# Layer 0 experts: three nested levels of token rounds per expert in place of eight, with the tokens beyond the 192nd in a block behind the last expert

## The chip, the cores and the metric

The kernel runs on one core of a Trainium2 chip. The time is that of one execution on the device, in microseconds (us); of several runs the median is given.

## The reference, cut to what matters

The program is a stack of two transformer blocks. In each of two layers of the first one, a mixer is followed by a mixture of experts, which is where the change is. Layer 0 sends 512 tokens through it (256 of the context, 256 of the sequence), layer 1 256 tokens:

```
g_sel = argmax(h @ grp_w + grp_b)                      # one of 4 groups per token
e_p, e_i = top_k(softmax(e_logits of that group), 2)   # two of its 8 experts
for each of 32 experts, over the tokens sent to it:
    hid = silu(xb @ w_gate[e]) * (xb @ w_up[e])        # 1024 -> 512
    out[token] += (hid @ w_down[e]) * weight           # 512 -> 1024
```

How many tokens an expert gets depends on the data; with 512 tokens and two experts each, the mean is 32, and up to 512 are possible. The result has to be right for any number.

## The kernel before, in words

**Experts.** `experts` goes through the 32 experts of a layer one after the other, in eight quads (`ORDER`) of four (`GROUPS`). For each expert three weight tiles of 2 MB come from HBM: two with the gate and up columns (`egu`), one with the down rows (`edn`). `self.W` is the stream of weight tiles: SP issues each load when a slot is free, with at most 7 tiles held in layer 0 and 8 in layer 1.

**The first 32 tokens of each expert** are handled without any branch, four experts at a time: `quad_prep` gathers 32 tokens for each of the four. For each expert TensorE then does the gate and up products (64 matmuls, tile `g` from the slots `s`), ScalarE the silu and VectorE the product with up (`hid`), TensorE transposes `hid`, VectorE copies it out (`hT`, L2025), and TensorE does the down product (32 matmuls, `g` from `s` and `hT`). `fill` puts pieces of the previous quad's way back (`give`) between these.

**Further tokens** go in rounds. Between `hid` and its transpose, layer 0 has an If on the expert's count (`rounds`, L2135). Its body (`rest`) does one round of 32 slots for the tokens from 32 on, then, nested in it, an If for tokens from 64 on with a round of 64 slots, and so on up to 448: eight levels. A round (`round`) gathers its tokens, multiplies with the weights that are in the slots, and adds the result into `xT`; its `hid` is called `xg`. The four engines TensorE, ScalarE, VectorE and GpSimd each load the count (L2007) and each take the branch for themselves. An engine whose If isn't taken jumps over the code of all levels to an else block, which only brings its semaphores to where they would be. For TensorE alone, a hint on where the branch will go is issued at the start of the expert (L2008, and L2143 for the nested ones).

**Layer 1** has no If between experts. There one block behind the last expert (`late_rounds`) does all rounds: it is entered only if some expert has more than 32 tokens (the maximum is in `most`, written in `route`, L1854 to L1856), and then loads the weights of the experts concerned once more into the last three slots. SP takes part in this If too, since it issues those loads.

**Order.** TensorE's instructions go in the order in which they are written (`manual_schedule`); those of the other engines are ordered by a scheduler, which moves nothing into or out of an If. Behind the last expert's If come its transpose and down product, then the last `give`s, the late block in layer 1, and `finish`, which needs the next weights (`wcd` behind layer 0).

Of the kernel before, what the change touches and what calls it, by code (L numbers as in the profile page):

```python
# [14 lines left out]
ALU = mybir.AluOpType  # L15
AX = mybir.AxisListType
ET = mybir.EngineType
# [214 lines left out]

GROUPS = (1, 2, 0, 3)
ORDER = (0, 4, 1, 5, 2, 6, 3, 7)


class Slots:
# [16 lines left out]
class Stream:  # L254
# [29 lines left out]
    def next(self):  # L284
        if not self.ready:
            r, self.reserve = self.reserve, 0
            self.pump()
            self.reserve = r
        return self.ready.popleft()
# [7 lines left out]
class Kernel:  # L297
# [37 lines left out]
    def run(self):  # L335
        tc, nc, d = self.tc, self.nc, self.d
        with tc.tile_pool(name="keep", bufs=1) as keep, tc.tile_pool(name="slots", bufs=1) as slots:
# [24 lines left out]
            for l in range(2):  # L362
                W.cap = 7 + l
                for q in ORDER:
                    for e in self.experts_of(q):
# [177 lines left out]
    def ab(self):  # L543
        tc, nc, d = self.tc, self.nc, self.d
        with tc.tile_pool(name="ab", bufs=1) as pool, tc.tile_pool(name="ab_t", bufs=5) as self.tmp, \
# [65 lines left out]
            def conv():  # L611
# [39 lines left out]
                for c in range(4):  # L651
# [8 lines left out]
                    yield  # L660

            first, rest, mods = conv0(), conv(), self.mods(self.later)

            def pull(gen, n):
# [20 lines left out]
            for i in range(7):  # L685
# [8 lines left out]
                for m in range(2):  # L694
# [32 lines left out]
                    if i > NCONV:  # L727
                        pull(rest, AB_CONV)
# [45 lines left out]
            for n, _ in enumerate(attention()):  # L774
                if n >= A0 and n % AMOD == 0:
                    pull(mods, 1)
                pull(first, 1)
                pull(rest, 1 if n < AREST else 2)
# [865 lines left out]
    def route(self, l, c0, n, R, rw10, cnt, most, iota, mixed):  # L1644


        tc, nc, d = self.tc, self.nc, self.d
        nt = n // 128
# [39 lines left out]
        else:  # L1688
            mx, m_s = mixed
            W.keep_idle(0)  # L1690
            v = m_s[:, 2048:4096].bitcast(BF16).rearrange("p (i t f) -> p i t f", i=2, t=nt)
# [37 lines left out]
        for i, (r, s, e) in enumerate(streams):  # L1729
# [4 lines left out]
            for j in range(8):  # L1734
                if l == 1 and j % 4 == 0:
                    w = W.next()
                    wv = w.rearrange("p (k m) -> p k m", k=KT)
                if l == 0 and i == 0 and j % 2 == 0:
                    if j % 4 == 0:
                        w = self.W.next()  # L1740
# [18 lines left out]
                q = self.t([256], tag="q", bufs=3) if j else acc  # L1759
# [47 lines left out]
        g = L[:, :, 0:4]  # L1807
# [35 lines left out]
        rk = self.ps("rk")  # L1843
# [6 lines left out]
        nc.vector.scalar_tensor_tensor(R.rearrange("p t g e -> p (t g e)"), rk[:, :nt * 32], 1.0,  # L1850
                                       A.rearrange("p t g e -> p (t g e)"), op0=ALU.add, op1=ALU.mult)
        nc.vector.tensor_copy(cnt, rk[:, nt * 32:nt * 32 + 32])
        if l:
            top = self.t([1], tag="top")  # L1854
            nc.vector.tensor_reduce(top, rk[:, nt * 32:nt * 32 + 32], axis=AX.X, op=ALU.max)
            nc.vector.tensor_copy(most, top)  # L1856

        ge, gw = self.t([nt, 4], tag="ge"), self.t(s1, tag="gw")
        nc.vector.tensor_tensor(ge, g, gm.to_broadcast([P, nt, 4]), op=ALU.subtract)
# [128 lines left out]
    def experts(self, cnt, most):  # L1988
        tc, nc, nt, n = self.tc, self.nc, self.nt, self.n_
        eng = [ET.PE, ET.Activation, ET.DVE] + [ET.Pool] * (nt == 4)  # L1990
        cur, nxt = [], []
        for _ in self.quad_prep(ORDER[0], cur):
            pass
        gives = deque()
        for qi, q in enumerate(ORDER):
            prep = self.quad_prep(ORDER[qi + 1], nxt) if qi < 7 else iter(())
            ys = self.fx("ys")
            xt, ix = cur

            def fill():  # L2000
                if gives:
                    gives.popleft()()

            for i, (g, e) in enumerate(zip(GROUPS, self.experts_of(q))):
                w = [self.W.next() for _ in range(3)]
                if nt == 4:
                    v = nc.values_load(cnt[0:1, e:e + 1], engines=eng, min_val=0, max_val=n)  # L2007
                    tc.mark_branch_hint_location(f"more{e}", hint=self.more(v, 32), engines=[ET.PE])  # L2008
                o = self.fx("g")
                for k in range(KT):  # L2010
                    for j in range(4):
                        self.mm(o[32 * j:32 * j + 32, :256], xt[:, k, g * 32:g * 32 + 32],
                                w[k // 4][:, (k % 4) * 1024 + j * 256:(k % 4) * 1024 + j * 256 + 256], k == 0, k == KT - 1)
                h, hT = self.fx("hid"), self.fx("hT")
                nc.scalar.activation(out=h, in_=o[:, 0:128], func=AF.Silu)  # L2015
                nc.vector.tensor_tensor(h, h, o[:, 128:256], op=ALU.mult)  # L2016
                fill()
                next(prep, None)
                if nt == 4:
                    self.rounds(g, q, w, v, 32, f"more{e}")  # L2020
                if (i, qi) != (3, 7):
                    self.W.done(w[0]), self.W.done(w[1])
                tr = self.fx("g")
                self.tp(tr[:, 0:128], h)
                turned = nc.vector.tensor_copy(hT, tr[:, 0:128])  # L2025
                fill()
                if self.l == 1 and (i, qi) == (0, 1):
                    with tc.issue_after(turned.ins):
                        self.tables()
                y = self.fx("g")  # L2030
                for k in range(4):
                    for j in range(4):
                        self.mm(y[32 * j:32 * j + 32, :256], hT[:, k * 32:k * 32 + 32],
                                w[2][:, k * 1024 + j * 256:k * 1024 + j * 256 + 256], k == 0, k == 3)
                for j in range(4):
                    nc.scalar.copy(out=ys[32 * g:32 * g + 32, j * 256:j * 256 + 256], in_=y[32 * j:32 * j + 32, :256])  # L2036
                if (i, qi) != (3, 7):
                    self.W.done(w[2])
            for _ in prep:
                pass  # L2040
            yh, yl, back = self.fx("yh"), self.fx("yl"), self.fx("back")
            nc.vector.tensor_scalar(back, self.iota[:, :n], ix[:, 0:1], None, op0=ALU.is_equal)
            b = 1024 if qi < 7 else 256
            for c in range(0, 1024, b):
                x = slice(c, c + b)
                nc.scalar.activation(out=yh[:, x], in_=ys[:, x], func=AF.Copy, scale=ix[:, 10:11])
                nc.vector.scalar_tensor_tensor(yl[:, x], ys[:, x], ix[:, 10:11], yh[:, x].bitcast(F32), op0=ALU.mult, op1=ALU.subtract)
            for f in range(KT if qi < 7 else 0):
                x = slice(f * 128, f * 128 + 128)
                gives.append(lambda f=f, h=yh[:, x], l=yl[:, x], back=back: self.give(h, l, back, f, "g"))  # L2050
            cur, nxt = nxt, []
        while gives:
            gives.popleft()()
        if nt == 2:
            self.late_rounds(cnt, most, w, eng + [ET.SP])
        for t in w:
            self.W.done(t)
        self.finish(yh, yl, back)
# [70 lines left out]

        return (v + 1023 - base) // 1024  # L2130

    def rounds(self, g, q, w, v, base, label=None):

        tc = self.tc
        with tc.If(v > base, label=label):  # L2135
            self.rest(g, q, w, v, base, label)

    def rest(self, g, q, w, v, base, label=None):
        slots = 32 if base == 32 else 64
        after = base + slots  # L2140
        inner = f"{label}_{after}" if label and after < self.n_ else None
        if inner:
            self.tc.mark_branch_hint_location(inner, hint=self.more(v, after), engines=[ET.PE])  # L2143
        self.round(g, q, w, base, slots)
        if after < self.n_:
            self.rounds(g, q, w, v, after, inner)

    def round(self, g, q, w, base, slots):

# [57 lines left out]
    def late_rounds(self, cnt, most, w, eng):  # L2207

        tc, nc, d, l, n = self.tc, self.nc, self.d, self.l, self.n_
        top = nc.values_load(most[0:1, 0:1], engines=eng, min_val=0, max_val=n)  # L2210
        with tc.If(top > 32):
            for e in range(32):
                v = nc.values_load(cnt[0:1, e:e + 1], engines=eng, min_val=0, max_val=n)
                with tc.If(v > 32):
                    for t, ap in zip(w, (d["egu"][l, e, 0], d["egu"][l, e, 1], d["edn"][l, e])):
                        nc.sync.dma_start(out=t[:, :4096], in_=ap)
                    self.rest(e // 8, e % 8, w, v, 32)


# ---- launch: one core  # L2220
# [13 lines left out]
```

## Time and profile before

| | |
|---|---|
| median of 3 runs | 2650.49 us (2650.46 to 2654.11) |
| profiled execution | 2647.26 us |
| its span, first to last instruction | 2645.4 us |
| mean granted TensorE clock | 0.887 |
| TensorE matmul busy | 2107.6 us, 80% of the span |
| VectorE, ScalarE, GpSimd busy | 1173.4, 879.4, 390.8 us |
| read from HBM | 609.46 MB |

PE is TensorE's matmuls, PEld its weight loads, DVE VectorE, ACT ScalarE, POOL GpSimd, SP SyncE. A name with a q behind it (DVEq) is the engine's sequencer: branches, semaphores, register loads and DMA issues, which don't count as busy. The granted clock is the share of full speed that TensorE was given, 1.0 or 0.5 at any moment. Times in a row without a unit are us; durations marked ns or written with slashes (least/median/most) are ns. "idle before" is how long an engine stood idle before the instructions of a group, with what ended that time.

### The profile page before, as it was taken

To read this page: it belongs to the slowest core of one execution; us is meant where nothing else is said; L and a number is where in the kernel's file an instruction comes from. 1 tells how busy PE (TensorE), PEld (TensorE's weight loads), DVE (VectorE), ACT (ScalarE), POOL (GpSimd) and SP (SyncE) were. 2 spreads that over 40 slices of the span, in tenths; PEclk is the share of its full clock that TensorE was granted. 3 is DMA by queue.
4 is the path that set the end of the run, shared out by engine and by line. 5 is a ranking of instruction groups with operands and counts; after the bars stand their busy time and mean duration, and the time that the engine had idled before them with its cause. 6 is when DMAs were issued, how large, how long until landed. Compare 5 with 4: busy or idle time off the path is not lost. (4 is left out here: it accounts for less than half of the span.)

```text
span 2645.4 us, 47453 instructions
## 1 busy us (share of the span) xinstructions
PE 2107.6 (80%) x20113; PEld 1572.7 (59%) x20113; DVE 1173.4 (44%) x2419; ACT 879.4 (33%) x1859; POOL 390.8 (15%) x443
## 2 busy tenths in 40 slices
PE   6769978667767777768976666658998998998998
PEld 4444665334434444337643333327988998888998
DVE  4996542123222223236431111116866557666565
ACT  4115531111111111135332121214654444564543
POOL 1990010011111111123100000002022002012001
PEclk9879988778778788878988888888999999999999
DMA  7427264973773762544469999995434352433442
GB/s 307 179 112 288 106 231 186 383 307 160 300 323 151 301 273 114 238 197 157 170 266 427 426 427 427 427 426 200 154 128 163 156 216 102 187 128 128 192 160 80
DMA packets 44769, 615.19 MB, mean 233 GB/s; under 512 B 5232, under 2 KB 6288, under 8 KB 7152
## 3 DMA queue, kind: packets, MB, share of 16 engines
q1 hardware_dynamic: 42992, 606.29, 56.7%
q0 software_dynamic: 1264, 4.23, 0.5%
q8 instruction: 200, 3.28, 0.5%
q14 instruction: 169, 1.38, 0.2%
q10 hardware_dynamic: 144, 0.01, 0.0%
HBM read 609.46 MB, written 1.05 MB: 231 GB/s over the span
## 5 line engine op out<-in xcount | busy, mean ns | idle before, releaser
L305 PE MATMUL pj<-s,s 128*128 128x256 f32 (+1 forms) x6416 | 892.9, 298 | 64.8 <-DVE s L312 39.8
L305 PEld LDWEIGHTS pj<-s,s 128*128 128x128 f32 x6416 | 832.1, 195 | 109.5 <-DVE s L312 43.2
L305 PE MATMUL g<-s,s 128*32 128x256 f32 x4096 | 284.4, 432 | 120.3 <-DMA s<-in_egu 111.5
L312 DVE TENSOR_TENSOR s<-s,s 128x512 fp32r<-128x512 f32 (+3 forms) x298 | 334.0, 1145 | 86.6 <-ACT s L311 85.6
L311 ACT CAST s<-s 128x512 fp32r<-128x512 f32 (+2 forms) x304 | 272.3, 939 | 155.3 <-PE pj L305 112.8
L305 PEld LDWEIGHTS g<-s,s 128*32 128x32 f32 x4096 | 144.1, 124 | 259.5 <-DMA s<-in_egu 140.2
L305 PE MATMUL g<-s,hT 128*32 128x256 f32 x2048 | 187.6, 529 | 122.7 <-DVE hT L2025 56.6
L305 PEld LDWEIGHTS g<-s,hT 128*32 128x32 f32 x2048 | 85.5, 145 | 205.1 <-issue 121.5
L2036 ACT COPY ys<-g 32x256 f32<-32x256 f32 x256 | 92.9, 363 | 342.2 <-PE g L305 339.9
L1963 POOL TENSOR_TENSOR xT<-xT,give 128x256 f32<-128x256 f32 x138 | 96.5, 725 | 698.5 <-ACT give L1962 698.5
L1966 DVE SCALAR_TENSOR_TENSOR xT<-g,mod,xT 128x256 f32<-128x256 f32 x126 | 57.4, 479 | 292.0 <-PE g L305 291.2
L305 PEld LDWEIGHTS <-s 128*128 128x128 bf16 x2560 | 117.1, 105 | 2.8 <-issue 2.5
L2015 ACT ACTIVATE hid<-g 128x128 f32<-128x128 f32 x64 | 17.7, 277 | 279.8 <-PE g L305 279.7
L2016 DVE TENSOR_TENSOR hid<-hid,g 128x128 f32<-128x128 f32 x64 | 18.0, 282 | 191.2 <-ACT hid L2015 191.1
L1115 POOL TENSOR_TENSOR ms<-ms,h 128x256 f32<-128x256 f32 x35 | 36.3, 1037 | 385.6 <-ACT h L1111 385.5
L305 PE MATMUL m<-s,xt 128*32 128x256 f32 (+1 forms) x1024 | 85.6, 403 | 0.0
L618 DVE SCALAR_TENSOR_TENSOR y<-s,cols,y 128x512 f32<-128x512 f32 x60 | 82.0, 1403 | 1.0
L1966 DVE SCALAR_TENSOR_TENSOR xT<-m,mod,xT 128x256 f32<-128x256 f32 x160 | 65.6, 477 | 28.5 <-PE m L305 28.2
L608 POOL TENSOR_TENSOR y<-y,cv 128x512 f32<-128x512 f32 x47 | 76.6, 1630 | 1.8
L305 PE MATMUL g<-oh,s 128*128 128x128 bf16 x1024 | 73.2, 227 | 0.0
L1115 POOL TENSOR_TENSOR sc<-sc,xg 128x256 f32<-128x256 f32 x5 | 4.0, 793 | 460.7 <-PE g L305 460.3
L2180 ACT ACTIVATE xg<-m 128x128 f32<-128x128 f32 x22 | 6.1, 277 | 189.7 <-PE m L305 189.7
(448 smaller groups left out, 2634.8 us busy)
## 6 DMA issues: line engine op xcount, KB each, us to landing
s<-in_egu SPq DMA_DIRECT2D x128, 2048.0 KB, 16.4
s<-in_edn SPq DMA_DIRECT2D x64, 2048.0 KB, 18.7
s<-in_wf SPq DMA_DIRECT2D x32, 2048.0 KB, 8.2
s<-in_mod_w SPq DMA_DIRECT2D x20, 2048.0 KB, 8.5
s<-in_win SPq DMA_DIRECT2D x16, 2048.0 KB, 8.0
s<-in_mod_c SPq DMA_DIRECT2D x4, 2048.0 KB, 22.1
s<-in_cmp_w SPq DMA_DIRECT2D x4, 2048.0 KB, 10.1
s<-in_wo SPq DMA_DIRECT2D x4, 2048.0 KB, 7.9
```

The costliest lines, as they stand in the source:

```text
L305: self.nc.tensor.matmul(out, lhsT=lhsT, rhs=rhs, start=start, stop=stop)
L311: self.nc.scalar.copy(out=h, in_=src)
L312: (eng or self.nc.vector).tensor_tensor(l, src, h.bitcast(F32), op=ALU.subtract)
L608: nc.gpsimd.tensor_tensor(y[:, c], y[:, c], u, op=ALU.add)
L618: nc.vector.scalar_tensor_tensor(yc, glu[:, c, :, i:i + 256], w[:, c * 31 + i:c * 31 + i + 1], yc, op0=ALU.mult, op1=ALU.add)
L1115: (nc.gpsimd if k < 6 else nc.vector).tensor_tensor(state[0], state[0], s, op=ALU.add)
L1963: nc.gpsimd.tensor_tensor(x[:, s:e], x[:, s:e], t, op=ALU.add)
L1966: nc.vector.scalar_tensor_tensor(x[:, s:e], o[:, s:e], self.mod[self.l][:, 40 + f, r:r + 1], x[:, s:e], op0=ALU.mult, op1=ALU.add)
L2015: nc.scalar.activation(out=h, in_=o[:, 0:128], func=AF.Silu)
L2016: nc.vector.tensor_tensor(h, h, o[:, 128:256], op=ALU.mult)
L2036: nc.scalar.copy(out=ys[32 * g:32 * g + 32, j * 256:j * 256 + 256], in_=y[32 * j:32 * j + 32, :256])
L2180: nc.scalar.activation(out=h, in_=o[:, 0:128], func=AF.Silu)
```

## The change

In layer 0 the nested levels of an expert end at 192 tokens: the Ifs at 32, 64 and 128 stay, those at 192, 256, 320, 384 and 448 go. Tokens from the 192nd on are done in the block behind the last expert, which layer 1 has already. It now stands in both layers, with its own starting point for each (`EARLY`): in layer 0 one If on the largest count over 192, and inside it, for each of the 32 experts, an If on the count, a reload of the weights and the nested rounds from 192 to 512. So layer 0 needs the largest count too, a reduce and a cast on VectorE in `route`, and five engines load it and branch on it behind the last expert.

```
+EARLY = (192, 32)
...
-        if l:
-            top = self.t([1], tag="top")
-            nc.vector.tensor_reduce(top, rk[:, nt * 32:nt * 32 + 32], axis=AX.X, op=ALU.max)
-            nc.vector.tensor_copy(most, top)
+        top = self.t([1], tag="top")
+        nc.vector.tensor_reduce(top, rk[:, nt * 32:nt * 32 + 32], axis=AX.X, op=ALU.max)
+        nc.vector.tensor_copy(most, top)
...
                 if nt == 4:
-                    self.rounds(g, q, w, v, 32, f"more{e}")
+                    self.rounds(g, q, w, v, 32, EARLY[0], f"more{e}")
...
-        if nt == 2:
-            self.late_rounds(cnt, most, w, eng + [ET.SP])
+        self.late_rounds(cnt, most, w, eng + [ET.SP])
...
-    def rounds(self, g, q, w, v, base, label=None):
-
-        tc = self.tc
-        with tc.If(v > base, label=label):
-            self.rest(g, q, w, v, base, label)
-
-    def rest(self, g, q, w, v, base, label=None):
+    def rounds(self, g, q, w, v, base, end, label=None):
+
+        with self.tc.If(v > base, label=label):
+            self.rest(g, q, w, v, base, end, label)
+
+    def rest(self, g, q, w, v, base, end, label=None):
         slots = 32 if base == 32 else 64
         after = base + slots
-        inner = f"{label}_{after}" if label and after < self.n_ else None
+        inner = f"{label}_{after}" if label and after < end else None
         if inner:
             self.tc.mark_branch_hint_location(inner, hint=self.more(v, after), engines=[ET.PE])
         self.round(g, q, w, base, slots)
-        if after < self.n_:
-            self.rounds(g, q, w, v, after, inner)
+        if after < end:
+            self.rounds(g, q, w, v, after, end, inner)
...
         tc, nc, d, l, n = self.tc, self.nc, self.d, self.l, self.n_
+        base = EARLY[l]
         top = nc.values_load(most[0:1, 0:1], engines=eng, min_val=0, max_val=n)
-        with tc.If(top > 32):
+        with tc.If(top > base):
             for e in range(32):
                 v = nc.values_load(cnt[0:1, e:e + 1], engines=eng, min_val=0, max_val=n)
-                with tc.If(v > 32):
+                with tc.If(v > base):
                     for t, ap in zip(w, (d["egu"][l, e, 0], d["egu"][l, e, 1], d["edn"][l, e])):
                         nc.sync.dma_start(out=t[:, :4096], in_=ap)
-                    self.rest(e // 8, e % 8, w, v, 32)
+                    self.rest(e // 8, e % 8, w, v, base, n)
```

## Rows read from the trace of the kernel before

**Rows 1.** Busy time by stretch: layer 0's experts, layer 1's experts.

```profile
core 0: us, PE busy (x) PEld busy (x) DVE busy (x) ACT busy (x) POOL busy (x), PEclk, DMA share, GB/s
380.00:1175.00 795.00, 583.09 (x7522) 339.71 (x7525) 199.98 (x572) 139.87 (x344) 96.50 (x138) 0.81 0.60 246
1345.00:1788.00 443.00, 286.06 (x3637) 156.33 (x3636) 68.23 (x188) 92.36 (x237) 0.00 (x0) 0.86 0.99 419
```

**Rows 2.** TensorE's matmuls by group and shape, 380 to 1175 us (layer 0's experts).

```profile
line engine op names shapes xcount | busy us, mean ns | idle before us <-releasers
L305 PE MATMUL g<-s,s 128*32 128x256 f32 x2048 | 126.9, 403 | 0.3 <-issue 0.3
L305 PE MATMUL g<-s,hT 128*32 128x256 f32 x1020 | 112.9, 620 | 101.3 <-DVE hT L2025 47.0 <-issue 45.9 <-ACTq L2135 5.7
...
L308 PE MATMUL g<-c_ident,hid 128*128 128x128 f32 x32 | 11.7, 366 | 42.6 <-PEq L2135 36.7 <-issue 2.8 <-DVE hid L2016 2.0
```

**Rows 3.** The same view, 1345 to 1788 us (layer 1's experts).

```profile
L305 PE MATMUL g<-s,s 128*32 128x256 f32 x2046 | 157.4, 462 | 119.9 <-DMA s<-in_egu 111.5 <-SPq L2211 8.4
L305 PE MATMUL g<-s,hT 128*32 128x256 f32 x992 | 72.5, 441 | 21.3 <-DVE hT L2025 9.7 <-DMA s<-in_edn 8.7 <-issue 1.6
...
L308 PE MATMUL g<-c_ident,hid 128*128 128x128 f32 x31 | 9.8, 315 | 13.2 <-DVE hid L2016 13.2
```

**Rows 4.** Who waited for whom, 380 to 1175 us: total, times, longest.

```profile
DVE hT L2025 <- DVEq L2135: 90.2, 17, 6.5
...
ACT yh L2196 <- PE m L305: 55.1, 16, 4.0
...
DVE s L1939 <- DVEq L2135: 40.7, 8, 6.2
PE g L308 <- PEq L2135: 36.7, 23, 4.2
```

**Rows 5.** The Ifs of L2135 in the whole execution: duration, first and last start.

```profile
L2135 PEldq COMPARE_BRANCH  x58: 65/367/6103, 392.5 to 1166.6; - x58
...
L2135 DVEq EVENT_SEMAPHORE  x32: 21/21/21, 394.0 to 1171.7; - x32
```

**Rows 6.** L2135 on VectorE, 478 to 486 us: one skip.

```profile
L2135 DVEq COMPARE_BRANCH  x1: 69/69/69, 478.6 to 478.6; - x1
L2135 DVEq EVENT_SEMAPHORE  x1: 21/21/21, 484.9 to 484.9; - x1
...
  DVE hT L2025: 6.5, 1
```

**Rows 7.** L2135 on ScalarE, 478 to 486 us: a short skip.

```profile
L2135 ACTq COMPARE_BRANCH  x1: 55/55/55, 478.3 to 478.3; - x1
L2135 ACTq EVENT_SEMAPHORE  x1: 17/17/17, 478.7 to 478.7; - x1
```

**Rows 8.** L2135 on ScalarE, 584 to 592 us: its first long skip.

```profile
L2135 ACTq COMPARE_BRANCH  x1: 45/45/45, 585.1 to 585.1; - x1
L2135 ACTq EVENT_SEMAPHORE  x1: 17/17/17, 590.5 to 590.5; - x1
```

**Rows 9.** L2135 on ScalarE, 1096 to 1103 us: its last long skip.

```profile
L2135 ACTq COMPARE_BRANCH  x1: 50/50/50, 1097.1 to 1097.1; - x1
L2135 ACTq EVENT_SEMAPHORE  x1: 17/17/17, 1102.1 to 1102.1; - x1
```

**Rows 10.** L2135 on GpSimd, 555 to 565 us: a skip.

```profile
L2135 POOLq COMPARE_BRANCH  x1: 45/45/45, 558.2 to 558.2; - x1
L2135 POOLq EVENT_SEMAPHORE  x1: 17/17/17, 558.9 to 558.9; - x1
```

**Rows 11.** Timeline, an expert of layer 1: start, duration, instruction.

```profile
1372.97 3.66 PE L305 MATMUL g<-s,s 128*32 128x256 f32 x64
```

**Rows 12.** The If of layer 1's late block (L2211).

```profile
L2211 SPq EVENT_SEMAPHORE  x9: 17/17/17, 1764.9 to 1795.2; - x9
...
L2211 PEldq COMPARE_BRANCH  x1: 4232/4232/4232, 1792.1 to 1792.1; - x1
```

**Rows 13.** Timeline: TensorE's first matmul behind that If.

```profile
1796.87 0.55 PE L305 MATMUL g<-back,yh 128*128 128x256 f32 x1 [4.02 <-PEq L2211]
```

**Rows 14.** The largest count in layer 1's routing, L1855 and L1856.

```profile
L1855 DVE TENSOR_REDUCE top<-rk x1: 177/177/177, 1338.5 to 1338.5; 128x1 f32<-128x32 f32 x1
L1856 DVE CAST most<-top x1: 142/142/142, 1338.7 to 1338.7; 128x1 int32<-128x1 f32 x1
```

## The prediction

> **What bounds the kernel now.** I read the time by stages first, then what TensorE waits for in the stage that the change touches, then single events.
>
> The stage is layer 0's experts, 380 to 1175 us: 795 us of the span. TensorE is busy 583 us of it, at a mean granted clock of 0.81, and the DMA engines 0.60 [rows 1]. Layer 1's experts have no branch between experts and are bound otherwise: DMA share 0.99 at 419 GB/s [rows 1]. So in layer 0 neither TensorE nor the transfers are full; something makes TensorE wait.
>
> TensorE's matmuls by group tell what [rows 2, 3]. In layer 0 the gate-and-up matmuls (g<-s,s) wait 0.3 us in all for their weights, but the down matmuls (g<-s,hT) find the engine idle for 101.3 us and the transpose of hid for 42.6 us. In layer 1 the same groups lose 21.3 us (8.7 of it to a DMA) and 13.2 us. The list of waits names the branch of L2135: VectorE's copy hT stood 90.2 us behind VectorE's own branch in 17 experts, another of its instructions 40.7 us in eight, and TensorE's transpose 36.7 us behind TensorE's [rows 4].
>
> How many experts skip? Each engine took 58 branches and 32 else blocks at L2135 [rows 5], and yh of a round ran 16 times [rows 4]. 58 is 32 outer Ifs, 16 nested ones (one behind each round) and one jump over the other else blocks in each expert with rounds: 58 - 32 - 16 = 10 such experts. So 22 of 32 experts skip all rounds. Their skip is what costs: VectorE branches at 478.6 and does the first thing behind it, the else block's semaphore, at 484.9, 6.3 us later, with hT waiting 6.5 us [rows 6].
>
> Whether a skip costs anything depends on the engine. ScalarE's took 0.4 us in one expert and 5.4 in another; eight of its 22 were long, the first and the last of them shown [rows 7 to 9]. GpSimd's took 0.7 us [rows 10], and all but one were as short. What differs is the code skipped. Counted in the compiled program of before, from branch to else block, it is about 234 instructions on VectorE, 150 on ScalarE, 72 on GpSimd and 3,365 on TensorE. Near targets are free, far ones cost 5 to 6 us, and in between it is chance.
>
> [...]
>
> **The change part by part.**
>
> *Five nested levels leave each expert.* Rounds from 192 up were never run here (one expert went three rounds, to 192), so no executed work goes; the skip gets shorter. Each level is 29 or 30 instructions on VectorE, so its skip falls from 234 to some 85, ScalarE's from 150 to 56, GpSimd's from 72 to 27, TensorE's from 3,365 to 1,280. 85 lies next to GpSimd's 72 (1 long of 22) and below ScalarE's 150 (8 of 22). Between them in proportion, 1 + 7 x 13/78, about 2 of 22 VectorE skips stay long. Bounds: 1 and 8.
>
> What goes: idle before the down matmuls 101.3 us, less what layer 1 shows without branches and its DMA (12.6 us in 31 experts, 13 in 32): 88 us. It includes the skips behind executed rounds, which get shorter too. With 2 of 22 kept: 80 us (bounds 84 and 56).
>
> *The clock.* The down matmuls, right behind the hold, average 620 ns in layer 0 and 441 in layer 1: 112.9 us for 1,020 against 72.5 for 992, so 38 us if they ran as there [rows 2, 3]. The gate-and-up group took 126.9 us; at 3.66 us for 64, as in one expert of layer 1 [rows 11], 32 would take 117: 10 us. [...] Bounds 0 and 48. I take three quarters, 36 us, since TensorE's own holds (next) stay in about a quarter of the experts.
>
> *TensorE's own skips.* Their branch took up to 6.1 us [rows 5]. The transpose's 36.7 us in 23 places [rows 4], less 0.43 each as in layer 1 (13.2 in 31), leaves 27 us, at up to 4.2 each some seven experts in which it is late, and hT's delay hides behind that. The hint (L2008) stays. No row shows a TensorE skip of 1,280, so I bound it by nothing gained and by all that layer 1 does without: 42.6 - 13.6 = 29 us. I take nothing: 1,280 is far beyond every jump that the rows show as free.
>
> *What comes next: the weights.* Layer 1's TensorE is busy 286 us for 31 experts, 9.2 each [rows 1], so an expert without rounds would take about 9 us, while its three tiles of 2 MB take 15 at 419 GB/s. Four tiles are buffered (cap 7, three in use), 20 us of transfer, and such experts come in runs of three at most; three run 3 x 6 = 18 us ahead. So the buffer just about covers it. Bounds 0 and 20; I take 10 us.
>
> *The block behind the last expert* is one If, not taken, over code for 32 experts on five engines. Layer 1 has it: TensorE's branch took 4.23 us, and the first matmul behind it came after 4.02 us idle [rows 12, 13], but most of that ran while ScalarE emptied the last down matmuls, which layer 0's end does too. I take half, 2 us (bounds 0 and 4.2; a VectorE skip runs beside it, not on top). Queued behind it: TensorE's last gives, VectorE's yl, ScalarE's ys, GpSimd's sums, and on SP the next weights. SP's else block lets nothing pass until the transfers ahead have landed: in layer 1 its semaphores went from 1764.9 to 1795.2 [rows 12]. In layer 0 what waits there is wcd, wanted only at the stage's end, and the expert before the last runs a round, in which no transfer is due. So nothing; without that cover it would cost the landing of three tiles, 15 us. SP also loads `most` before the experts and waits there for the routing, when the slots are full and no load could go.
>
> *The routing* gets the reduce and the cast on VectorE: 0.18 + 0.14 = 0.3 us [rows 14], on the path.
>
> Sum: 80 + 36 - 10 - 2 - 0.3 = 103.7 us. The profiled execution took 2647.26 us, so 2543.6; the median of the runs shown (2650.49) is 3.2 above that execution: **2547 us**.
>
> **The rivals.**
>
> *TensorE's late skips go too.* For: the skip shrinks to 38% there as well. Against: layer 1's TensorE branch, without a hint, stalls, and nothing shows where free ends on that engine. Then 29 us more and the whole 48 of the clock, less 14 for weights: 80 + 29 + 48 - 14 - 2.3 = 141, so 2510 us.
>
> [...]
>
> *TensorE's skips take VectorE's place.* hT no longer waits, but more transposes do, as experts follow faster. If all 22 lost 3.4 us, 15 more than now, 51 us return and the clock stays low: 80 - 51 - 5 - 2.3 = 22, so 2629 us. For: these holds are in the list of waits already. Against: hint and branch stay the same distance apart in TensorE's code.
>
> *A skip costs a refetch however short.* Then VectorE's holds stay, nothing is won, and the block at the end is paid in full: 4.2 + 0.3 us, and 1.2 more if the last down matmuls' share of the clock (38 us over 32 experts) is lost once more: 2653 to 2656 us. It decides if VectorE's 85 behaves like its 234. For: every VectorE skip looked at is long. Against: GpSimd's and most of ScalarE's aren't.
>
> **How the numbers follow.** Forecast 0.50 (its own range 2520 to 2575, from the bounds above), TensorE's skips go 0.27, they take over 0.16, refetch however short 0.07. The forecast is the likeliest case. The range runs from 2500, the second case with a few us to spare, to 2600, between the forecast and the third, of which about a third lies inside: some 0.82. A change under 0.2% (5 us) can't be told from none. Faster 0.93 (the first three), same 0.03 and slower 0.04 from the last, whose price straddles that bound.
>
> **What would show it.** Right: VectorE's wait before hT falls from 90 us to under 15; VectorE's else semaphore follows its branch within 1 us in about 20 skips; the down matmuls' mean falls toward 450 ns; the stage ends near 1072 us; gate-and-up matmuls begin to wait for in_egu, by some 10 us; one TensorE branch of 3 to 5 us appears behind the last expert. Wrong: hT still behind VectorE's branch, the transpose's wait grown past 50 us, or down matmuls still at 600 ns with the holds gone. What would make the figure wrong is chiefly TensorE's skips, of which no row shows one of the new length.

## The result and the profile after

The median went from 2650.5 to 2572.6 us (2569.3 to 2580.9 in four runs), a ratio of 0.971 (95% interval 0.969 to 0.972). That is 78 us, where 103.7 were forecast. The profiled execution took 2569.26 us.

The stage of layer 0's experts, from the first gate-and-up matmul to the last down matmul, went from 785.2 us (390.3 to 1175.5) to 711.2 (390.8 to 1102.0): 74 of the 78 us. The rest lies behind it and was not followed. The first view is the busy time by stretch, the columns as in [rows 1]:

```profile
core 0: us, PE busy (x) PEld busy (x) DVE busy (x) ACT busy (x) POOL busy (x), PEclk, DMA share, GB/s
380.00:1105.00 725.00, 563.30 (x7527) 333.66 (x7527) 205.19 (x579) 140.81 (x349) 96.71 (x138) 0.86 0.65 269
1272.00:1715.00 443.00, 286.82 (x3625) 154.71 (x3623) 68.84 (x190) 92.62 (x238) 0.00 (x0) 0.85 0.99 421
```

TensorE's mean granted clock is 0.86 where it was 0.81 [rows 1]; layer 1's stage is as it was. TensorE's matmuls by group, answering [rows 2]:

```profile
L307 PE MATMUL g<-s,s 128*32 128x256 f32 x2048 | 129.3, 400 | 6.5 <-issue 6.1 <-DVE oh L1975 0.3
L307 PE MATMUL g<-s,hT 128*32 128x256 f32 x1024 | 97.1, 533 | 21.4 <-DVE hT L2026 13.0 <-issue 7.7 <-ACTq L2134 0.7
...
L310 PE MATMUL g<-c_ident,hid 128*128 128x128 f32 x32 | 12.0, 374 | 62.3 <-PEq L2134 55.3 <-DVE s L1940 3.6 <-DVE hid L2017 2.0
```

The idle time before the down matmuls fell from 101.3 to 21.4 us, that before the transpose rose from 42.6 to 62.3, and the down matmuls take 533 ns where they took 620. By the record of the granted clock 994 of the 1,024 down matmuls started at its lower level before (626 ns each on average), and 613 do after; those at the higher level take 393 ns. In the list of waits, of the 90.2 us of hT behind VectorE's branch [rows 4] 2.9 us are left, of the 40.7 us of s 0.3; what remains is TensorE behind its own branch, 36.7 us before:

```profile
PE g L310 <- PEq L2134: 55.3, 24, 6.2
```

One skip shows both engines; it answers to [rows 6]. The If of L2134 on VectorE and on TensorE's sequencer, 732 to 741 us:

```profile
L2134 DVEq COMPARE_BRANCH  x1: 56/56/56, 733.2 to 733.2; - x1
L2134 DVEq EVENT_SEMAPHORE  x1: 21/21/21, 733.7 to 733.7; - x1
...
L2134 PEldq COMPARE_BRANCH  x1: 6538/6538/6538, 732.6 to 732.6; - x1
```

VectorE passes in 0.5 us, TensorE's branch takes 6.5. In the timeline the transpose comes after 6.2 us idle:

```profile
739.35 0.45 PE L310 MATMUL g<-c_ident,hid 128*128 128x128 f32 x1 [6.20 <-PEq L2134]
```

Counted over the 22 experts that skip, branch to else block: VectorE was late (over 1.5 us) in 22 before, median 5.7 us, and in none after, at most 0.6. ScalarE went from six to none, GpSimd from one to none. TensorE's 22 branches took 54.4 us together before and 76.8 after, with 15 and 21 of them over 0.5 us. The block behind the last expert shows as expected, answering to [rows 12, 13]; its If on TensorE, 1095 to 1106 us:

```profile
L2211 PEldq COMPARE_BRANCH  x1: 3337/3337/3337, 1101.0 to 1101.0; - x1
```

and the first matmul behind it in the timeline:

```profile
1104.82 0.47 PE L307 MATMUL g<-back,yh 128*128 128x512 f32 x1 [2.81 <-PEq L2211]
```

### The profile page after: what moved, and what is told of

Same layout as the page of the kernel before. It is cut to its first block, busy times and chain, and to the rows that moved or that the text cites. A ratio compares the mean times of both kernels' runs of the same rounds, so it can differ in the third digit from the quotient of the medians.

```text
span 2567.4 us, 47473 instructions
## 1 busy us (share of the span) xinstructions
PE 2082.9 (81%) x20113; PEld 1562.8 (61%) x20113; DVE 1178.7 (46%) x2421; ACT 878.8 (34%) x1859; POOL 391.3 (15%) x443
## 5 line engine op out<-in xcount | busy, mean ns | idle before, releaser
L307 PE MATMUL g<-s,hT 128*32 128x256 f32 x2048 | 171.3, 486 | 41.9 <-DVE hT L2026 23.2
L307 PEld LDWEIGHTS g<-s,hT 128*32 128x32 f32 x2048 | 79.5, 133 | 116.0 <-issue 66.9
L310 PE MATMUL g<-c_ident,hid 128*128 128x128 f32 x64 | 22.2, 347 | 76.2 <-PEq L2134 55.3
L610 POOL TENSOR_TENSOR y<-y,cv 128x512 f32<-128x512 f32 x47 | 76.6, 1630 | 1.8
```

Source lines behind the costliest of these rows:

```text
L307: self.nc.tensor.matmul(out, lhsT=lhsT, rhs=rhs, start=start, stop=stop)
L310: self.nc.tensor.transpose(out, in_, self.ident)
L610: nc.gpsimd.tensor_tensor(y[:, c], y[:, c], u, op=ALU.add)
```

## What TensorE's late branch is

The trace records the packets that bring instructions: 16 KB each on queue q8, 8 KB each on q14. By kind, over the stage, before and after (packets, MB, share of the 16 engines):

```profile
q8 instruction: 98, 1.61, 0.8%
q14 instruction: 123, 1.01, 0.4%
```

```profile
q8 instruction: 92, 1.51, 0.8%
q14 instruction: 54, 0.44, 0.2%
```

More than half of the packets on q14 are gone with the change (123 to 54), those on q8 are not (98 to 92). In after, 21 of TensorE's 22 branches end 1.4 to 1.6 us behind the end of a 16 KB packet, so those are taken here as TensorE's, and those on q14 as the other engines'. Read from the records, for four skips of after and two of the run light_weights below (us; the last column is the DMA engines' busy share with other transfers between hint and packet):

```
                     branch  late by  hint ahead by  packet starts  share
after, 1st expert     393.0    2.16       2.4        2.0 after hint  0.00
after, 5th            476.5    6.19       4.7        8.4             0.99
after, 17th           732.6    6.54       4.7        8.7             1.00
after, 24th           907.4    1.75       4.3        3.6             1.01
light_weights, 17th   695.9    2.18       4.7        4.6             0.77
light_weights, 24th   846.8    0.46       3.7        1.0             0.21
```

In 11 of the 22 skips of after, another 16 KB packet starts between the hint and the packet that ends the branch, in nine of them within 1.4 us behind the hint; these 11 branches take 4.8 us on average, the others 2.2. Before the change there were four such skips. On average the hint came 5.7 us ahead of the branch before and 5.5 after, but the packet that ends the branch started 5.6 us behind the hint before and 6.4 after, at a DMA share of 0.94 and 0.93. So the fetch behind the hint got slower, beside equally busy DMA engines. That the first of two such packets is the code that follows in order is the author's guess; no trace shows it.

Theory 1: a skip out of the code at hand waits for one fetch of the code behind it; on TensorE the hint starts it early, weight transfers hold it up, and VectorE's holds used to give it time. On VectorE the length of the skip decides whether a fetch is needed. Rivals: TensorE's cost depends on its skip's length; the fetch takes its time whatever else is transferred; the gain came from fewer levels or shorter TensorE code, not from VectorE's skip.

## The experiments

A ratio is to the kernel before, with its 95% interval; after has 0.971 (0.969 to 0.972). "Sum" is the time of TensorE's 22 branches, "transpose" and "down" the idle time before these matmuls, "stage" layer 0's experts, all in us.

```
                 sum   transpose  down   down matmul ns  stage   median
before          54.4     42.6    101.3        620        785.2   2650.5
after           76.8     62.3     21.4        533        711.2   2572.6
dve_pad         48.0     31.2    100.9        606        767.4   2631.3
pe_pad          73.8     55.6     25.4        539        730.1   2583.5
no_hint        133.3    113.7     21.2        598        774.5   2632.6
hint_early      60.9     70.6     17.5        542        720.3   2579.8
load_early      65.3     61.2     18.9        539        708.3   2569.9
light_weights   24.2     19.2     18.1        461        636.0   2498.8
before_light    22.5     19.1     70.2        568        720.1   2574.5
one_level       49.1     36.0     32.5        508        556.5   2415.2
five_levels     59.7     41.5     45.0        548        719.6   2585.4
split4          76.6     60.1     15.3        551        723.7   2577.9
split2          78.0     61.7     14.8        517        712.8   2572.6
no_late         75.8     61.9     22.2        526        712.3   2570.8
```

**dve_pad: VectorE's length alone put back.**

```
+        elif label:
+            with self.tc.If(v > after):
+                pad = self.fx("oh2")
+                for _ in range(140):
+                    self.nc.vector.tensor_scalar(pad[:, 0, :64], self.iota[:, :64], self.R[:, 0, g, q:q + 1], None, op0=ALU.is_equal)
```

> Kernel after, with 140 VectorE instructions more in an If over 192 tokens, nested behind the third level, that is never taken. VectorE's skip is as long as before the change again (some 230 instructions), TensorE's stays at 1,280, ScalarE's and GpSimd's grow by five. Theory 1 (what the change won is the length of VectorE's skip): VectorE's first instruction behind its branch comes 5 to 6 us late in some 20 experts, idle time before the down matmuls goes from 21 us back to 85 to 105, the transpose's idle time falls from 62 to about 40 since TensorE's fetch then hides, and the time is 2630 to 2655 us. Rival (it is the number of levels or TensorE's shorter code): 2570 to 2585 us, hT waits for nothing.

Ratio 0.993 (0.991 to 0.995), in the range of theory 1. 140 instructions that never run take back 59 of the 78 us. VectorE was late in 21 of 22, median 5.5 us. TensorE's groups in the stage:

```profile
L307 PE MATMUL g<-s,hT 128*32 128x256 f32 x1024 | 110.3, 606 | 100.9 <-issue 52.3 <-DVE hT L2026 48.7
L310 PE MATMUL g<-c_ident,hid 128*128 128x128 f32 x32 | 11.4, 355 | 31.2 <-PEq L2134 28.2 <-DVE hid L2017 2.0
```

and the list of waits:

```profile
DVE hT L2026 <- DVEq L2134: 79.0, 16, 6.1
DVE s L1940 <- DVEq L2134: 37.2, 7, 6.2
PE g L310 <- PEq L2134: 28.2, 24, 4.3
```

The down matmuls' idle time is that of [rows 2] again, and their slow 606 ns with it. But for the added If TensorE's code is that of after, yet its sum falls from 76.8 to 48.0 us: with VectorE's hold back TensorE's fetch lands earlier. The lead of the hint is as in after (5.4 us on average), the packet starts 5.1 us behind it where it took 6.4, and a second packet comes in between in two skips where it was 11. That the hold lets the code that follows in order land before the next hint is the reading that fits these counts, and no run shows it. The rival (levels, or TensorE's code) falls.

**pe_pad: TensorE's length alone put back.**

```
+        elif label:
+            with self.tc.If(v > after):
+                pad = self.fx("m")
+                for _ in range(522):
+                    self.mm(pad[0:32, :256], w[0][:, 0:32], w[0][:, 0:256], True, True)
```

> Kernel after, with 522 matmuls more (2,088 TensorE instructions) in an If over 192 tokens, nested behind the third level, that is never taken. TensorE's skip is 3,377 instructions, as before the change; the other engines' skips grow by five at most. Theory 1 (a TensorE skip costs one fetch whatever its length beyond the near code): as after, 2568 to 2580 us, the transpose's idle time 55 to 68 us. Rival (a long skip costs TensorE more than one of 1,280, so the change did win something there): the transpose's idle time 75 to 100 us, time 2590 to 2610 us.

Ratio 0.974 (0.972 to 0.976): 11 us above after, between the two expectations. The transposes are as theory 1 has them, at 55.6 us:

```profile
L310 PE MATMUL g<-c_ident,hid 128*128 128x128 f32 x32 | 11.9, 373 | 55.6 <-PEq L2134 49.7 <-PEq L2147 3.2 <-DVE hid L2017 2.0
```

The extra time stands largely elsewhere, in the group of the gate-and-up matmuls (129.3 to 138.3 us busy, 6.5 to 12.1 idle):

```profile
L307 PE MATMUL g<-s,s 128*32 128x256 f32 x2048 | 138.3, 422 | 12.1 <-issue 11.8 <-DVE oh L1975 0.3
```

"Issue" says that no recorded instruction held them. But the six gaps of over 0.5 us there (11.8 us in all) end 1.3 to 1.5 us behind the end of a 16 KB packet, as the late branches do, and so do the four in after (6.1 us; before had none): TensorE seems to wait for code there too. Why pe_pad has more of them stays open. Length itself, from 1,280 to 3,377, costs TensorE's skip nothing (sum 73.8 us, in after 76.8).

**no_hint: the outer hint taken out.**

```
-                    tc.mark_branch_hint_location(f"more{e}", hint=self.more(v, 32), engines=[ET.PE])
```

> Kernel after without the hint of L2009 on where each expert's outer branch goes; the hints of the nested Ifs stay. Theory 1 (TensorE's late branch is a fetch of the code behind the skip, which the hint starts some 2 to 9 us ahead of the branch, and which then waits behind the weight transfers): without it each of the 22 skips pays the whole fetch, 5 to 6.5 us where it pays 0.4 to 6.5 now (77 us in all); the branches' sum goes to 115 to 140 us, the time to 2605 to 2630 us. The ten taken Ifs pay nothing. Rival (the hint does nothing, the fetch starts at the branch anyway): 2568 to 2580 us, branches as now.

Ratio 0.993 (0.991 to 0.995). The sum, 133.3 us, is as theory 1 has it, the time 2.6 us above its range. Every one of the 22 is late: the first and the last, with a DMA share of 0.02 and 0.03 during the branch, by 3.7 us, the others by 5.8 to 7.4. TensorE's groups:

```profile
L307 PE MATMUL g<-s,hT 128*32 128x256 f32 x1024 | 110.6, 598 | 21.2 <-DVE hT L2025 14.6 <-issue 6.5
L310 PE MATMUL g<-c_ident,hid 128*128 128x128 f32 x32 | 13.5, 423 | 113.7 <-PEq L2133 113.7
```

The clock follows the holds, whoever causes them: the down matmuls are at 598 ns with VectorE free, 909 of them at the lower level.

**hint_early and load_early: the hint one expert ahead.** In hint_early TensorE loads the next expert's count and gives the hint right behind the present If; in load_early all four engines load it one expert earlier still, so that only the hint stands there.

```
                     self.rounds(g, q, w, v, 32, EARLY[0], f"more{e}")
+                    if len(hinted) < 32:
+                        hint(order[len(hinted)])           # hint_early
+                        hint(order[len(hinted)], ahead)    # load_early
```

> Kernel after with TensorE's hint for the next expert issued right behind this expert's If, ahead of its transpose and down product, with a register load of its own on TensorE. It is 4 to 5 us earlier. Theory 1 (the fetch starts with the hint and lands 5 to 14 us later, behind the weight transfers): the branches' sum falls from 77 us to under 35, the transpose's idle time from 62 to under 30, the time to 2525 to 2550 us. Rival (an early hint is lost, because the next sequential fetch comes between it and the branch): branches as now or longer, 2565 to 2620 us.

> As hint_early, but the counts are loaded one expert ahead on all four engines (at the start of the expert before), so that behind the If only the hint itself stands, without the register load that cost TensorE's transpose some 2 us in each expert there. Theory 1 (an earlier hint brings the fetch forward by 1 to 1.5 us, no more, since the next sequential fetch goes first): branches' sum 55 to 65 us, transpose's idle time 40 to 50 us, time 2553 to 2568 us. Rival (the earlier hint wins nothing, the sum in hint_early was shorter because the transposes were late anyway): sum 70 to 80 us, time 2570 to 2580 us.

Ratios 0.973 (0.971 to 0.974) and 0.970 (0.968 to 0.972): nothing won. The hint of load_early was meant to give the fetch 4 us more; the sum went down by 11.5 us in all, and the transpose's idle time hardly moved. Theory 1's size was wrong here: the hint came 8.8 us ahead on average where it came 5.5, but the packet started 9.2 us behind it where it took 6.4, and in 15 of the 22 skips another packet came in between. So the lead is not what is short. In hint_early the register load in front of the transpose costs what the sum gained (its idle time is 70.6 us, 51.2 of it put down to issue).

**light_weights: a quarter of the weight traffic.**

```
+                        c = 4096 if l else 1024
-                        W.add(d["egu"][l, e, 0], 4096)
+                        W.add(d["egu"][l, e, 0][:, :c], c)
...
-w[k // 4][:, (k % 4) * 1024 + j * 256: ...
+w[k // 4][:, (k % 4) * 1024 * self.l + j * 256: ...
```

> Kernel after, but of each weight tile of layer 0's experts only the first 1,024 of 4,096 columns are loaded (512 KB in place of 2 MB), and the matmuls read those columns in place of the rest: three quarters of the expert weights of layer 0 are left out. Number and length of the instructions stay. Theory 1 (TensorE's fetch of the code behind the skip stands behind the weight transfers: the two skips of after without or with late transfers started 2.0 and 2.3 us behind the hint, the others 3.6 to 11.5 at a DMA share of 1.0): the 22 branches' sum falls from 77 us to under 30, the transpose's idle time from 62 to under 20 us, the time to 2505 to 2535 us. Rival (the fetch takes its time whatever else the DMA engines do): sum 65 to 85 us, transpose's idle time 55 to 65, time 2560 to 2575 us.

The time, 2498.8 us, is below even theory 1's. The sum is 24.2 us, the branch's share of the transpose's idle time 11.3 where it was 55.3, and the down matmuls are at 461 ns, 332 of them at the lower level. TensorE's groups:

```profile
L307 PE MATMUL g<-s,hT 128*32 128x256 f32 x1024 | 80.9, 461 | 18.1 <-DVE hT L2027 12.3 <-issue 4.5 <-ACTq L2135 1.1
L310 PE MATMUL g<-c_ident,hid 128*128 128x128 f32 x32 | 10.8, 337 | 19.2 <-PEq L2135 11.3 <-DVE oh L1976 3.0 <-DVE hid L2018 2.7
```

and the stage's row by stretch, the columns as in [rows 1]:

```profile
391.00:1027.00 636.00, 531.48 (x7418) 322.80 (x7418) 200.61 (x559) 137.69 (x340) 96.92 (x138) 0.90 0.25 83
```

Same instructions, same skips, DMA share 0.25 where it was 0.66 (390.8 to 1102.0 us): the late fetch is a matter of the transfers around it, and the rival falls.

**before_light: the same edit on the kernel before.**

> Kernel before with the edit of light_weights: of each weight tile of layer 0's experts only 1,024 of 4,096 columns are loaded and read again in place of the rest, so three quarters of those weights are left out; all skips as long as before the change. Theory 1 (VectorE's late skip is a fetch from memory too, which stands behind the weight transfers: the first skip, with no transfer in flight, was late by 3.0 us, the others by 5 to 6): VectorE stays late in about 22 skips, but by some 3 us each, the idle time before the down matmuls falls from 101 us to 50 to 65, and the time is 2535 to 2565 us, 35 to 65 above light_weights. Rival (the 5 to 6 us are the price of the jump, whatever is transferred): idle time 85 to 105 us, time 2570 to 2600 us.

VectorE is late in 22 of 22 still, but by 2.9 us (median) where it was 5.7. So its long skip is a fetch behind the transfers too. The time (2574.5) lies in the rival's range and the down idle time (70.2 us) between the two; theory 1 hadn't counted the skips behind executed rounds, which are late too, by 2.8 to 3.9 us in all ten experts that have them. Its group of down matmuls and its longest wait for a branch:

```profile
L305 PE MATMUL g<-s,hT 128*32 128x256 f32 x1024 | 102.6, 568 | 70.2 <-issue 36.8 <-DVE hT L2026 30.9 <-ACT s L311 2.6
```

```profile
DVE hT L2026 <- DVEq L2136: 49.8, 16, 4.8
```

With a quarter of the traffic the change is worth 2574.5 - 2498.8 = 76 us: half the price for each late skip on VectorE, but nothing given back on TensorE (sum 22.5 and 24.2 us).

**split4 and split2: the same bytes in smaller packets.**

```
+            step = w // parts
+            for c in range(0, w, step):
+                self.nc.sync.dma_start(out=t[:, c:c + step], in_=ap[:, c:c + step])
-            self.nc.sync.dma_start(out=t[:, :w], in_=ap)
```

> Kernel after, with each 2 MB weight tile of layer 0's experts loaded by four DMAs of 1,024 columns in place of one: the same bytes in packets of 4 KB (159 ns each in light_weights) in place of 16 KB (611 ns each in after). Theory 1 (TensorE's fetch waits for some packets of the weights ahead of it, so their size sets the wait; in light_weights the fetch started 1.8 to 2.9 us behind the hint even at a DMA share of 0.9 and more): the 22 branches' sum falls from 77 us to 25 to 45, the transpose's idle time from 62 to under 40 us, layer 0's experts from 711 to 655 to 685 us, the time to 2520 to 2550 us. Rival (light_weights won by the time in which nothing was transferred, not by its packets): sum 65 to 85 us, time 2565 to 2580 us.

> As split4 with two DMAs of 2,048 columns for each tile, packets of 8 KB. Theory 1: between after and split4, branches' sum 40 to 60 us, time 2540 to 2565 us. Rival: as after, sum 65 to 85 us, 2565 to 2580 us.

Ratios 0.972 (0.970 to 0.974) and 0.970 (0.967 to 0.972), sums 76.6 and 78.0 us: as the rival has it, and theory 1 falls in this form. The packets were 4 and 8 KB (159 and 311 ns each), so it isn't their size that the fetch waits for. What in the traffic holds it up stays open.

**five_levels and one_level: other lengths.**

```
-EARLY = (192, 32)
+EARLY = (320, 32)     # five_levels
+EARLY = (64, 32)      # one_level, and late_rounds only in layer 1
```

> Kernel after with the Ifs at 192 and 256 put back (five levels, late block from 320 on). VectorE's skip is some 150 instructions, as ScalarE's was before the change, which was late in 8 of 22 experts; ScalarE's is 100, GpSimd's 50, TensorE's 2,120. Theory 1 (VectorE's length decides, TensorE's doesn't): VectorE late in 5 to 12 of 22, time 2585 to 2612 us, TensorE's branches as after or better hidden. Rival (between 85 and 234 nothing happens until 200): VectorE late in none, 2570 to 2583 us.

> Kernel after with only the If at 32 left in each expert of layer 0 and no late block there: the rounds for tokens beyond the 64th of an expert are left out (six rounds of 64 slots in this data, some 23 to 26 us each, so 140 to 160 us less work). TensorE's skip goes from 1,280 to some 445 instructions, VectorE's from 85 to 25. Theory 1 (any TensorE target beyond the code at hand is one fetch): the 22 skips' branches sum to 60 to 90 us, as the 77 of after. Rival (the length decides on TensorE too, as on VectorE): they sum to under 25 us.

five_levels: ratio 0.975 (0.973 to 0.977), at theory 1's lower end; VectorE was late in three of the 22 (5.4 to 5.7 us), fewer than the five at least that theory 1 gave, and behind rounds as well. Its waits:

```profile
PE g L310 <- PEq L2134: 37.9, 24, 5.6
DVE hT L2026 <- DVEq L2134: 20.2, 6, 5.9
```

one_level is a single run, and with rounds left out its time can't be compared. Its sum of 49.1 us meets neither number. Skips of 445 instructions on TensorE were late by up to 5.9 us, 17 of them by over 0.5; five of the seven with no transfer between hint and packet took 0.4 to 0.5. So a short skip isn't free there; how much of the smaller sum is length and how much is other timing of the transfers wasn't separated. Here the weights' bound shows that after never met, in the list of waits:

```profile
PE g L307 <- DMA s<-in_egu: 16.9, 7, 3.6
```

**no_late: the block behind layer 0 left out.**

```
-        self.late_rounds(cnt, most, w, eng + [ET.SP])
+        if nt == 2:
+            self.late_rounds(cnt, most, w, eng + [ET.SP])
```

> Kernel after without the block behind layer 0's last expert, so that tokens beyond the 192nd of an expert are left out (there are none in this data). Theory 1 (the block costs what TensorE idles behind its branch, 2.8 us in after, less what ScalarE's copies hold it anyway, 2.2 us in before): 0.5 to 3 us less than after, 2569 to 2573 us, no branch of 3 us behind the last expert. Rival (it also delays the next stage's weights or the other engines): 5 us less or more, 2563 to 2568 us.

Ratio 0.969 (0.9675 to 0.9705), 1.8 us under after, the intervals overlapping. There TensorE's first matmul behind the last expert waits 2.17 us for yh; with the block it waits 2.81 for the branch. Its timeline:

```profile
1107.67 0.50 PE L307 MATMUL g<-back,yh 128*128 128x512 f32 x1 [2.17 <-ACT yh L2047]
```

## Why the prediction was right, and where it was off

The time fell inside the range, and at the slow end of the forecast's own. One of the signs of being wrong came too: the transpose's wait grew past 50 us.

*VectorE's holds, 80 us: right.* 101.3 - 21.4 = 79.9 us, and dve_pad shows that it is VectorE's length. That the number is met so closely is luck: two late skips were kept, for 8 us, and none stayed late, but 21.4 us of idle time are left where 13 were taken as what stays anyway, with at most 2.9 of them behind VectorE's branch. ScalarE's late skips were six of 22, not eight. The rival "A skip costs a refetch however short" falls with the 22 else blocks that come within 0.6 us.

*TensorE's own skips, nothing: this step failed.* They cost 62.3 - 42.6 = 19.7 us more. The argument was that 1,280 is as far beyond the free jumps as 3,365, and pe_pad bears that out; what it missed is that TensorE's fetch had been landing earlier with VectorE's hold there (dve_pad: 48.0 us with it, 76.8 without). So the rival "TensorE's skips take VectorE's place" was the mechanism, at 20 us and not at the 51 it was priced with, beside the forecast's gain and not in place of it. The objection to it, that hint and branch stay the same distance apart, held even of the time (5.7 and 5.5 us); what grew is the time from the hint to the packet. "TensorE's late skips go too" is out, since their sum rose.

*The clock, 36 us: mechanism right, size off.* The down matmuls gave back 112.9 - 97.1 = 15.8 us, and the gate-and-up group's busy time grew by 2.4 us (at 400 ns each where it was 403): 13 us. No run shows the forecast's 36 us: 613 of the 1,024 down matmuls still started at the lower level, where it was 994. The three quarters assumed TensorE's holds in some seven experts, a quarter; its branch took over 0.5 us in 15 of the 22 skips before the change already, and does in 21 after it. When light_weights took most of that away, the down matmuls went to 461 ns, near layer 1's 441 [rows 3].

*The weights, 10 us lost: not met.* TensorE never waits for in_egu. It idles 6.2 us more before the gate-and-up matmuls, put down to issue, in gaps that end behind its instruction packets (see pe_pad). That late skips kept the experts slow enough for the buffer is likely, but no run tests it.

*The late block, 2 us:* 1.8 by no_late, which the overlapping intervals don't tell from nothing.

Together 79.9 + 13.4 - 19.7 - 6.2 = 67 us of the stage's 74; small differences in other groups make the rest.

## What to carry to other kernels

Code that never runs can cost time if a branch must jump over it. On VectorE 140 such instructions cost 59 us (dve_pad), on TensorE 2,088 more cost the skip nothing (pe_pad), so look at every engine's branch-to-else time by itself before shortening what it skips. Before counting a removed stall in full, ask what was landing under it; here a second engine's fetch came later without it and gave a quarter of the gain back (19.7 of 79.9 us). A hold showed twice here, as idle time and as slower matmuls behind it (101.3 us and 620 ns before, 21.4 us and 533 ns after), and a stall that another engine took over kept the clock low too (no_hint: 113.7 us before the transpose, and down matmuls at 598 ns).

## What the runs showed that was not expected

Whether a skip of middle length is late is no chance: ScalarE's six late skips were in the same six experts in before and before_light, and GpSimd's one in the same expert. By length, late among 22: VectorE 85 instructions 0, 150 three, 230 to 234 21 and 22; ScalarE 56 and 100 none, 150 six; GpSimd 72 one. What decides in which experts a skip of 72 or 150 instructions is late, no run shows.

A late skip that nothing hints at took 2.9 and 3.1 us on VectorE (before) and 3.7 on TensorE (no_hint) in the first and the last of the 22, at a DMA share of 0.00 and of 0.02 and 0.03, and in the others 5.3 to 6.3 us (share 0.54 to 0.99) and 5.8 to 7.4; making the weights' packets four times smaller changed nothing (split4: sum 76.6 us, in after 76.8).
